# Decoder layer on one core: where three modulation segments are loaded and summed, and where the last projection group adds its partial sums

## The chip, the cores and the metric

The kernel runs on one core of one Trainium2 chip, as one launch. The time is the device time of that core in microseconds (us), the median of several runs. One further execution was recorded by the hardware profiler; the profile and the trace are of that execution.

## The reference

One layer of a decoder trunk in float32, 256 rows (tokens) of 2048 channels:

- `mod = silu(c) @ w_ada + b_ada`, cut into six segments of 2048: shift1, scale1, gate1, shift2, scale2, gate2. `w_ada` is 2048 x 12288, so one segment is 16 MB of weights for one row of result.
- `h = rms_norm(x) * (1 + scale1) + shift1`, and `proj = h @ w_in`. The columns of `proj` feed three token mixers (stick-breaking attention, dilated attention, gated linear attention, called GLA below) and three sigmoid branch gates of 2048 columns each.
- `y` = sum over the three branches of gate times (mixer output @ its branch weights); `x = x + gate1 * (y @ w_out)`.
- `h2 = rms_norm(x) * (1 + scale2) + shift2`; `x = x + gate2 * ((silu(h2 @ w_gate) * (h2 @ w_up)) @ w_ffn_out)`.

So gate1 is first needed when `y @ w_out` is there, shift2 and scale2 directly after it, gate2 at the very end.

## The kernel before

**A block.** All large products run as blocks of 512 output columns. Every float32 operand is split into a high part and a remainder, and each product is three matmuls (`mm3`, L149: high x high, high x low, low x high; their trace lines are L150, L151, L152). A block over 16 slices of 128 input channels (k) and two halves of 128 rows (t) is 96 matmuls. Its weights come in pieces of two k slices, 512 KB each (`load_weights`, L122): a DMA on SP's queue into a buffer `raw` (four of them), ScalarE (ACT) copies out the high part `whi` (L144), VectorE (DVE) subtracts for `wlo` (L145). The sums stand in the PSUM pool `acc` of four banks; a block takes two, one for each t. A second PSUM pool, `misc`, has four banks too.

**Order.** Each engine's instructions run in an order that is fixed when the kernel is built. It is set by priorities and by a modelled readiness: `prio()` (L98) moves what it holds 4000 steps ahead of its place in the program text, so weight loads, splits and evacuations of the accumulators come as soon as their buffers allow, and the blocks' matmuls fill PE's time between the matmuls of the mixers. `tc.issue_after(x)` keeps an instruction behind x on its engine. SP, ACT and DVE each work strictly through their own list; a DMA whose buffer is not free yet holds up all DMAs behind it on SP's list.

**Stages.** 36 us of start; then the first 13 blocks of `w_in` (tiles `A0` to `A12`) in four groups of k slices (`GROUPS`, L38), because the modulation (shift1, scale1) of a group of channels must be there first: in each group every block is run over that group's k alone and its sum is added to `A[b]` by DVE (`proj_block`, L386; the addition is L402). The last group has five k slices, 30 matmuls a block. Its blocks are traced in the order 0 to 4, then stick-breaking attention, then `gla()` (L532: the 16-column decay input first, in a bank of `acc`; blocks 9 to 12; the GLA chain), then blocks 5 to 8, then `dilated()` (L644). Only then comes the middle stage: two blocks for the GLA output gate, twelve gate blocks (`gate_block`, L779) and four `y_block`s (L850), then four blocks of `w_out` (the fourth with its weights kept, one t after the other, L938 to L947), then the FFN.

**The background.** The 16 MB of each later segment are streamed by a generator, `ada_segment_steps` (L307): one step issues one 512 KB load of `w_ada` into a ring buffer (`araw`), and, as many steps later as the ring has buffers, DVE multiplies that piece by silu(c) and adds it to the segment's accumulator (`ada_mac`, L242; its trace line is L247; "a mac" below). A mac is issued after the latest split that has been traced (`state["split"]`), which, as `block` traces all its splits first, is the last split of the current block. `block` calls `tick` once for every two k slices; `state["rate"]` says how many background steps a tick makes: nothing in the four groups, 0.8 in the middle stage (`RATE_MID`), 0.4 in the FFN. The background of the middle stage (L710) does gate1, then shift2, then scale2, each one whole before the next: 32 loads, then the sums over the 128 partitions on PE. For shift2 and scale2 these are 16 products with a column of ones (`column_sum`, L289, traced as L290); for gate1 (`gate_rows`, L728) the bias is added, and products with a 128 x 128 matrix of ones give every row the sum. Before the fourth `w_out` block `flush()` (L939) runs all background that is left.

Of the kernel before, what the change touches and what calls it, by code (L numbers as in the profile page):

```python
# [10 lines left out]
F32 = mybir.dt.float32  # L11
# [6 lines left out]
P = 128  # L18
T = 256
# [46 lines left out]
def trunk(ctx: ExitStack, tc: tile.TileContext, I, out):  # L66
# [38 lines left out]

    state = {"rate": 0.0}
    bg = []
    later = []

    def tick(n):  # L110
        state["due"] = state.get("due", 0.0) + n
        while state["due"] >= 1.0:
            state["due"] -= 1.0
            if bg and next(bg[0], "end") == "end":
                bg.pop()

    def flush():
        while bg:
            tick(1)


# [24 lines left out]
                parts += [(hi[:, i, :], lo[:, i, :]) for i in range(n)]  # L146
        return parts

    def mm3(ps, lh, ll, rh, rl, start, stop):  # L149
        nc.tensor.matmul(ps, lh, rh, start=start, stop=False)  # L150
        nc.tensor.matmul(ps, lh, rl, start=False, stop=False)  # L151
        state["mm"] = nc.tensor.matmul(ps, ll, rh, start=False, stop=stop)  # L152

    def block(pss, act, src, k0, k1, c0, base=0, w=None, tiles=range(NT), go_on=False, more=False):

        if w is None:
            w = load_weights(src, k0, k1, c0)
        for k in range(k0, k1):
            if (k - k0) % 2 == 0 and tiles[-1] == NT - 1:
                tick(state["rate"])  # L160
            if k - k0 == DEFER and later:
                with tc.issue_after(state["mm"].ins), prio():
                    later.pop()()
            wh, wl = w[k - k0]
            for t in tiles:
                h, l = act(base + k, t)
                mm3(pss[t], h, l, wh, wl, k == k0 and not go_on, k == k1 - 1 and not more)

    def split_from_psum(hi, lo, ps):
        nc.scalar.copy(hi, ps)  # L170
# [133 lines left out]
        ring["n"] += 1  # L304
        return S(ring["tags"][ring["n"] % len(ring["tags"])], shape, dtype)

    def ada_segment_steps(acc, seg):  # L307

        steps = [(k, j) for k in range(KC) for j in range(2)]
        lag = len(ring["tags"])  # L310
        raws = []

        def mac(i):
            k, j = steps[i]
            with tc.issue_after(state["split"].ins):
                ada_mac(acc[j], raws[i], k)

        for i, (k, j) in enumerate(steps):
            if i >= lag:
                mac(i - lag)  # L320
            raw = araw([P, 2 * NB])
            c0 = seg * D + j * 2 * NB
            with prio():
                nc.sync.dma_start(raw, w_ada[k * P : (k + 1) * P, c0 : c0 + 2 * NB])
            raws.append(raw)
            yield
        for i in range(len(steps) - lag, len(steps)):
            mac(i)
            yield


# [51 lines left out]
    orders = (up[1:] + up[:1], up, down)  # L383
    carried = []

    def proj_block(g, b, w=None, carry=False):  # L386
        k0, k1 = GROUPS[g]
        go_on = bool(carried)
        pss = carried.pop() if go_on else [acc_bank() for _ in range(NT)]
        block(pss, h_at, w_in, k0, k1, b * NB, w=w, go_on=go_on, more=carry)  # L390
        if carry:
            carried.append(pss)
            return
        with prio():
            first = A[b] is None
            if first:
                A[b] = S(f"A{b}", [P, NT, NB])
            for t in range(NT):
                if first:
                    nc.scalar.copy(A[b][:, t, :], pss[t])  # L400
                else:
                    nc.vector.tensor_add(A[b][:, t, :], A[b][:, t, :], pss[t])  # L402
# [30 lines left out]
    for g in range(len(GROUPS) - 1):  # L433
# [7 lines left out]
        for _ in nxt:  # L441
            pass
        h_group(g + 1)
    LAST = len(GROUPS) - 1


    kc = S("KC", [P, 8, P])
# [83 lines left out]

    def gla():  # L532
        aw = load_weights(w_in, 0, KC, COL_A, P)
        ps = acc_bank([P, T])
        for k in range(KC):
            hh = hT[0][k // 4][:, k % 4, :]
            hl = hT[1][k // 4][:, k % 4, :]
# [169 lines left out]
        return oT  # L707


    def background():  # L710
        state["gate1"] = yield from gate_rows(SEG_GATE1)
        state["mod2"] = []
        for seg in (SEG_SHIFT2, SEG_SCALE2):
            acc = [S(f"T{4 + j}", [P, 2 * NB]) for j in range(2)]
            yield from ada_segment_steps(acc, seg)
            v = const.tile([P, KC], F32, name=nm("mod2"))
            for i in range(0, KC, 4):
                ps = misc_bank([P, 4])
                for j in range(4):
                    q = (i + j) % 8  # L720
                    with tc.issue_after(state["mm"].ins):
                        column_sum(ps[:, j : j + 1], acc[(i + j) // 8][:, q * P : (q + 1) * P])
                    if j % 2:
                        yield
                finish_columns(ps, v[:, i : i + 4], seg, i, ROW_N2 if seg == SEG_SCALE2 else None)
            state["mod2"].append(v)

    def gate_rows(seg):  # L728
        acc = S("ada", [P, D])
        yield from ada_segment_steps([acc[:, : 2 * NB], acc[:, 2 * NB :]], seg)  # L730
        for j in range(4):
            c = slice(j * NB, (j + 1) * NB)
            br = scr([1, NB])
            nc.sync.dma_start(br, I["b_ada"][:, seg * D + c.start : seg * D + c.stop])
            nc.vector.tensor_add(acc[0:1, c], acc[0:1, c], br)
            yield
        for _ in range(4):
            yield
        for j in range(4):
            c = slice(j * NB, (j + 1) * NB)  # L740
            hl = araw([P, 2, NB], F32R)
            hi, lo = hl[:, 0, :], hl[:, 1, :]
            nc.scalar.copy(hi, acc[:, c])
            nc.vector.tensor_tensor(lo, acc[:, c], hi.bitcast(F32), op=ALU.subtract)
            yield
            ps = misc_bank([P, NB])
            with tc.issue_after(state["mm"].ins):
                nc.tensor.matmul(ps, ones_r, hi, start=True, stop=False)
                nc.tensor.matmul(ps, ones_r, lo, start=False, stop=True)
            nc.scalar.copy(acc[:, c], ps)  # L750
            yield
        return acc
# [143 lines left out]
    def residual(n, t, ps):  # L896

        xr = x2[n][:, t, :]
        tmp = scr([P, NB])
        nc.vector.tensor_mul(tmp, gate1[:, n * NB : (n + 1) * NB], ps)  # L900
# [39 lines left out]
    sh2, sc2 = state["mod2"]  # L940
# [16 lines left out]
    w_ff = I["w_ffn_in"]  # L957

    def gate2_bg():
        state["gate2"] = yield from gate_rows(SEG_GATE2)  # L960

    state["rate"] = RATE_FFN
    ring["tags"] = ("AR0", "AR1", "KC")
# [36 lines left out]
    def add_out(n, t, ps, pieces=1):  # L1000

        w = NB // pieces
        for a in range(0, NB, w):
            tmp = scr([P, w])
            c0 = n * NB + a
            nc.vector.tensor_mul(tmp, gate2[:, c0 : c0 + w], ps[:, a : a + w])
# [51 lines left out]
```

## Time and profile before

| | before |
|---|---|
| median of 3 runs | 1651.34 us (1651.2 to 1651.47) |
| profiled execution: its own time | 1653.2 us |
| profiled execution: span, first to last instruction | 1651.4 us |
| PE matmul busy | 1605.1 us, 97% of the span |
| DVE busy | 1136.2 us, 69% |
| ACT busy | 773.0 us, 47% |
| data moved | 395.91 MB, mean 240 GB/s |

A busy time is the sum of an engine's recorded instructions. PE's matmuls overlap (each is recorded as about 390 ns long, and one starts every 226 ns or so), so PE can be recorded as busy while it makes less progress than it could: the number of matmuls in a stretch is the better measure. "PEclk" is the share of full speed that PE's clock was granted. "Idle before" is the time that an engine stood still ahead of an instruction, with what ended it.

### The profile page before, as it was taken

What the parts mean: (1) busy time and instruction counts of PE and PEld (TensorE: products, weight loads), DVE (VectorE), ACT (ScalarE), POOL (GpSimd) and SP (SyncE); (2) the same over time, 40 slices, a digit from 0 to 9 for tenths busy, and PEclk for the clock granted to TensorE, in tenths of its full rate; (3) what the DMA queues carried; (4) which work ended last, traced back from release to release, by engine and by line L of the source; (5) the groups of instructions that cost most, each with busy time, mean ns of one, the idle gap of its engine ahead of it and who ended that gap; (6) DMA issues with size and microseconds to landing.
All of it is one profiled execution on the core that took longest, in us unless ns stands there. A gap on an engine that the chain in (4) does not pass through costs nothing.

```text
span 1651.4 us, 19878 instructions
## 1 busy us (share of the span) xinstructions
PE 1605.1 (97%) x7293; PEld 1324.2 (80%) x7293; DVE 1136.2 (69%) x1367; ACT 773.0 (47%) x1073; POOL 6.0 (0%) x14
## 2 busy tenths in 40 slices
PE   3999999999999999899998999999999999999998
PEld 3788888888878887688887788888888888888887
DVE  5789997787888476866987556766755555554453
ACT  5554446556755444344444644444444444433332
POOL 1000000000000000000000000000000000000000
PEclk8999999999999999999999999999999999999999
DMA  8899986445698778987997467877666566565663
GB/s 299 311 320 323 330 286 217 140 140 166 219 314 296 230 230 309 310 276 263 324 313 268 151 229 258 269 255 258 234 191 190 181 190 192 190 202 194 206 207 111
DMA packets 194561, 395.91 MB, mean 240 GB/s; under 512 B 12898, under 2 KB 27912, under 8 KB 194464
## 3 DMA queue, kind: packets, MB, share of 16 engines
q1 hardware_dynamic: 194240, 394.63, 71.9%
q8 instruction: 57, 0.93, 0.2%
q14 instruction: 40, 0.33, 0.1%
q0 software_dynamic: 224, 0.01, 0.0%
HBM read 392.50 MB, written 2.10 MB: 239 GB/s over the span
## 4 chain that ended last, share of the span: by engine, by line
PE 82%; DMA 7%; DVE 6%; issue 2%; ACT 2%; SPq 1%; DVEq 0%; ACTq 0%
PE acc L150 26%; PE acc L151 26%; PE acc L152 26%; DVE wlo L145 2%; DVE T L247 2%; DMA raw<-w_in 2%; DMA raw<-w_out 2%; ACT whi L144 1%; PE misc L592 1%; PE misc L290 1%; PE misc L846 1%; DVE ada L247 1%; DMA A<-x 1%; DMA raw<-w_br_gla 0%; DMA OS<-w_ada 0%
## 5 line engine op out<-in xcount | busy, mean ns | idle before, releaser
L145 DVE TENSOR_TENSOR wlo<-raw,whi 128x1024 fp32r<-128x1024 f32 (+1 forms) x548 | 653.3, 1197 | 422.2 <-ACT whi L144 420.1
L144 ACT CAST whi<-raw 128x1024 fp32r<-128x1024 f32 (+1 forms) x548 | 563.8, 1032 | 734.2 <-PE acc L152 555.4
L151 PE MATMUL acc<-wlo,H 128*128 128x512 f32 x1576 | 617.7, 392 | 1.7 <-DVE wlo L145 1.7
L150 PE MATMUL acc<-whi,H 128*128 128x512 f32 x1576 | 616.4, 392 | 2.5 <-ACT whi L144 2.5
L152 PE MATMUL acc<-whi,H 128*128 128x512 f32 x1576 | 616.8, 392 | 0.0
L151 PEld LDWEIGHTS acc<-wlo,H 128*128 128x128 f32 x1576 | 297.0, 189 | 64.3 <-DVE wlo L145 4.0
L150 PEld LDWEIGHTS acc<-whi,H 128*128 128x128 f32 x1576 | 296.8, 188 | 64.4 <-ACT whi L144 3.4
L152 PEld LDWEIGHTS acc<-whi,H 128*128 128x128 f32 x1576 | 296.8, 188 | 62.7 <-DVE H L372 0.9
L150 PE MATMUL acc<-whi,A 128*128 128x512 f32 x312 | 123.1, 396 | 2.7 <-ACT whi L144 2.7
L151 PE MATMUL acc<-wlo,A 128*128 128x512 f32 x312 | 123.1, 395 | 1.7 <-DVE wlo L145 1.7
L152 PE MATMUL acc<-whi,A 128*128 128x512 f32 x280 | 110.2, 394 | 0.0
L150 PEld LDWEIGHTS acc<-whi,A 128*128 128x128 f32 x312 | 59.1, 190 | 15.5 <-ACT whi L144 3.5
L151 PEld LDWEIGHTS acc<-wlo,A 128*128 128x128 f32 x312 | 59.5, 191 | 15.0 <-DVE wlo L145 2.9
L152 PEld LDWEIGHTS acc<-whi,A 128*128 128x128 f32 x280 | 53.4, 191 | 11.2
L402 DVE TENSOR_TENSOR A<-A,acc 128x512 f32<-128x512 f32 x72 | 47.9, 684 | 10.2 <-PE acc L152 10.0
L150 PE MATMUL acc<-whi,T 128*128 128x512 f32 x120 | 46.7, 389 | 0.0
L151 PE MATMUL acc<-wlo,T 128*128 128x512 f32 x120 | 46.7, 389 | 0.0
L152 PE MATMUL acc<-whi,T 128*128 128x512 f32 x120 | 46.7, 389 | 0.0
L247 DVE SCALAR_TENSOR_TENSOR ada<-AR,csil,ada 128x1024 f32<-128x1024 f32 x35 | 44.2, 1278 | 0.8 <-DMA AR<-w_ada 0.8
L152 PE MATMUL acc<-whi,OS 128*128 128x512 f32 x112 | 43.6, 389 | 0.0
L247 DVE SCALAR_TENSOR_TENSOR T<-AR,csil,T 128x1024 f32<-128x1024 f32 x30 | 38.1, 1277 | 0.0
L247 DVE SCALAR_TENSOR_TENSOR ada<-OS,csil,ada 128x1024 f32<-128x1024 f32 (+2 forms) x33 | 35.5, 1074 | 1.4 <-DMA OS<-w_ada 1.2
(323 smaller groups left out, 1198.5 us busy)
## 6 DMA issues: line engine op xcount, KB each, us to landing
raw<-w_in SPq DMA_DIRECT2D x205, 512.0 KB, 4.8
raw<-w_ffn_in SPq DMA_DIRECT2D x176, 512.0 KB, 3.7
raw<-w_ffn_out SPq DMA_DIRECT2D x88, 512.0 KB, 4.7
AR<-w_ada SPq DMA_DIRECT2D x69, 512.0 KB, 4.7
KC<-w_ada SPq DMA_DIRECT2D x35, 512.0 KB, 5.9
raw<-w_out SPq DMA_DIRECT2D x32, 512.0 KB, 7.0
KD<-w_ada SPq DMA_DIRECT2D x24, 512.0 KB, 5.6
OS<-w_ada SPq DMA_DIRECT2D x16, 512.0 KB, 6.3
```

Of the source, the lines that this page charges most:

```text
L144: nc.scalar.copy(hi[:, :n, :], raw[:, :n, :])
L145: state["split"] = nc.vector.tensor_tensor(lo[:, :n, :], raw[:, :n, :], hi[:, :n, :].bitcast(F32), op=ALU.subtract)
L150: nc.tensor.matmul(ps, lh, rh, start=start, stop=False)
L151: nc.tensor.matmul(ps, lh, rl, start=False, stop=False)
L152: state["mm"] = nc.tensor.matmul(ps, ll, rh, start=False, stop=stop)
L247: nc.vector.scalar_tensor_tensor(acc, raw, c, acc, op0=ALU.mult, op1=ALU.add)
L290: nc.tensor.matmul(ps, acc, ones[:, 0:1], start=True, stop=True)
L402: nc.vector.tensor_add(A[b][:, t, :], A[b][:, t, :], pss[t])
L592: nc.tensor.matmul(ps[:, h, :], at(lhs, h, t), at(rhs, h, t), start=True, stop=True)
L846: nc.tensor.transpose(ps[:, i, :], src[:, i * P : (i + 1) * P], ident)
```

## The change

- The background starts before the last group. Its rate is still 0 for blocks 0 to 4; from the stick-breaking attention on it is 0.8 (`RATE_IN`), which makes it run during the last group's blocks 9 to 12 and 5 to 8 with a ring of two buffers. In the middle stage, with four buffers, the rate is 0.6.
- The order is shift2, gate1, scale2, as one unbroken stream of loads: a segment's sums over partitions go into a second list, `after`, of which each tick makes a step as well, so that they run beside the next segment's loads. Column sums start four steps after the segment's last mac. gate1 and gate2 are kept as four quarters, summed in pieces of 256 columns through the tile `T6`. gate1 now stands in `T4` and `T5`, shift2 and scale2 in `ada`.
- In the last group, blocks 1 to 12 (block 0 goes on from the group before) start from their sum so far: ACT copies `A[b]` into the two PSUM banks ahead of the block ("a seed"), all matmuls accumulate onto it, and ACT copies the banks back into `A[b]`. DVE's additions of these blocks are gone.
- The decay input of `gla()` uses a bank of `misc` instead of `acc`. The first FFN block keeps its late weights in other tiles.

```diff
-RATE_MID, RATE_FFN = 0.8, 0.4
+RATE_IN, RATE_MID, RATE_FFN = 0.8, 0.6, 0.4
...
+            for work in (bg, after):
+                if work and next(work[0], "end") == "end":
+                    work.pop(0)
...
+    macs = []
+    def mac():
+        acc, j, k, raw, done = macs.pop(0)
+        with tc.issue_after(state["split"].ins):
+            ada_mac(acc[j], raw, k)
+        if done is not None:
+            after.append(done)
+    def ada_segment_steps(acc, seg, done):
+        for k in range(KC):
+            for j in range(2):
+                while len(macs) >= len(ring["tags"]):
+                    mac()
+                raw = araw([P, 2 * NB])
...
+                macs.append((acc, j, k, raw, done if (k, j) == (KC - 1, 1) else None))
+                yield
+    def last_macs():
+        while macs:
+            mac()
             yield
...
-        block(pss, h_at, w_in, k0, k1, b * NB, w=w, go_on=go_on, more=carry)
+        seeded = g == LAST and not go_on
+        if seeded:
+            with prio():
+                for t in range(NT):
+                    nc.scalar.copy(pss[t], A[b][:, t, :])
+            go_on = True
+        block(pss, h_at, w_in, k0, k1, b * NB, w=w, go_on=go_on, more=carry, seeded=seeded)
...
-                if first:
+                if first or seeded:
                     nc.scalar.copy(A[b][:, t, :], pss[t])
                 else:
                     nc.vector.tensor_add(A[b][:, t, :], A[b][:, t, :], pss[t])
...
-        ps = acc_bank([P, T])
+        ps = misc_bank([P, T])
...
+    def columns(seg, acc):
+        for _ in range(4):
+            yield
+        v = const.tile([P, KC], F32, name=nm("mod2"))
+        for i in range(0, KC, 4):
+            ps = misc_bank([P, 4])
+            for j in range(4):
+                with tc.issue_after(state["mm"].ins):
+                    column_sum(ps[:, j : j + 1], acc[:, (i + j) * P : (i + j + 1) * P])
+                if j % 2:
+                    yield
...
+    def background():
+        for seg in (SEG_SHIFT2, SEG_GATE1, SEG_SCALE2):
+            if seg == SEG_GATE1:
+                acc = [S(f"T{4 + j}", [P, 2 * NB]) for j in range(2)]
+                yield from ada_segment_steps(acc, seg, rows_of("gate1", seg, acc))
+            else:
+                acc = S("ada", [P, D])
+                yield from ada_segment_steps(halves(acc), seg, columns(seg, acc))
+        yield from last_macs()
+    bg.append(background())
     for b in range(0, 5):
         proj_block(LAST, b)
+    state["rate"] = RATE_IN
     sb_hi, sb_lo = stick_breaking()
...
-    bg.append(background())
...
-            w = load_weights(w_ff, 0, KC, 0, spare=("A12", "T4", "T5", "A9", "A10", "OD", "A1", "T1"))
+            w = load_weights(w_ff, 0, KC, 0, spare=("A12", "KD", "A9", "A10", "A0", "A1", "T1", "T2"))
```

More of the change, by code (lines that the diff above doesn't have):

```diff
@@ L113, in tick @@
             state["due"] -= 1.0
-            if bg and next(bg[0], "end") == "end":
-                bg.pop()
+            for work in (bg, after):
+                if work and next(work[0], "end") == "end":
+                    work.pop(0)
     def flush():
-        while bg:
+        while bg or after:
             tick(1)
@@ L147, in load_weights, with mm3, block @@
         return parts
[L149 to L154, printed above, removed]
+    def mm3(ps, lh, ll, rh, rl, start, stop, seeded=False):
+        nc.tensor.matmul(ps, lh, rh, start=start, stop=False, skip_group_check=seeded)
+        nc.tensor.matmul(ps, lh, rl, start=False, stop=False, skip_group_check=seeded)
+        state["mm"] = nc.tensor.matmul(ps, ll, rh, start=False, stop=stop, skip_group_check=seeded)
+    def block(pss, act, src, k0, k1, c0, base=0, w=None, tiles=range(NT), go_on=False, more=False, seeded=False):
         if w is None:
@@ L305, in araw @@
         return S(ring["tags"][ring["n"] % len(ring["tags"])], shape, dtype)
[L307 to L328, printed above, removed]
+    macs = []
[11 more added lines that the diff above has]
+                raw = araw([P, 2 * NB])
+                c0 = seg * D + j * 2 * NB
+                with prio():
+                    nc.sync.dma_start(raw, w_ada[k * P : (k + 1) * P, c0 : c0 + 2 * NB])
+                macs.append((acc, j, k, raw, done if (k, j) == (KC - 1, 1) else None))
[3 more added lines that the diff above has]
+            mac()
             yield
@@ L707, in dilated, with rows_of @@
         return oT
[L710 to L732, printed above, removed]
+    mod2 = {}
+    def columns(seg, acc):
[9 more added lines that the diff above has]
+                    yield
+            finish_columns(ps, v[:, i : i + 4], seg, i, ROW_N2 if seg == SEG_SCALE2 else None)
+        mod2[seg] = v
+    def rows_of(name, seg, acc):
+        quarters = [a[:, c : c + NB] for a in acc for c in (0, NB)]
+        for j, q in enumerate(quarters):
             br = scr([1, NB])
-            nc.sync.dma_start(br, I["b_ada"][:, seg * D + c.start : seg * D + c.stop])
-            nc.vector.tensor_add(acc[0:1, c], acc[0:1, c], br)
+            nc.sync.dma_start(br, I["b_ada"][:, seg * D + j * NB : seg * D + (j + 1) * NB])
+            nc.vector.tensor_add(q[0:1, :], q[0:1, :], br)
             yield
@@ L959, in gate2_bg @@
     def gate2_bg():
[L960 removed]
+        acc = halves(S("ada", [P, D]))
+        yield from ada_segment_steps(acc, SEG_GATE2, rows_of("gate2", SEG_GATE2, acc))
+        yield from last_macs()
     state["rate"] = RATE_FFN
```

40 lines of the change are left out of this document (22 added, 18 removed).

## The prediction

> **What bounds the kernel now.** I read the page first, then the busy time by stretches over the stages, then PE's waits.
>
> ```profile
> span 1651.4 us, 19878 instructions
> PE 1605.1 (97%) x7293; PEld 1324.2 (80%) x7293; DVE 1136.2 (69%) x1367; ACT 773.0 (47%) x1073; POOL 6.0 (0%) x14
> ```
>
> ```profile
> core 0: us, PE busy (x) PEld busy (x) DVE busy (x) ACT busy (x) POOL busy (x), PEclk, DMA share, GB/s
> 1500.00:1600.00 100.00, 100.00 (x443) 82.81 (x442) 49.94 (x45) 38.72 (x37) 0.00 (x0) 1.00 0.62 205
> 238.00:280.00 42.00, 42.00 (x196) 35.00 (x195) 35.70 (x66) 26.70 (x78) 1.75 (x1) 1.00 0.78 246
> 280.00:340.00 60.00, 60.00 (x313) 48.95 (x311) 41.18 (x75) 35.63 (x61) 0.00 (x0) 1.00 0.45 140
> 340.00:398.00 58.00, 57.88 (x321) 49.11 (x321) 54.44 (x75) 29.81 (x44) 0.00 (x0) 1.00 0.48 150
> 398.00:446.00 48.00, 47.79 (x225) 38.54 (x224) 35.54 (x93) 38.15 (x124) 0.00 (x0) 1.00 0.59 194
> 446.00:480.00 34.00, 32.41 (x156) 26.33 (x156) 29.05 (x49) 19.53 (x34) 0.00 (x0) 1.00 0.90 308
> 480.00:600.00 120.00, 120.00 (x539) 99.49 (x538) 87.97 (x92) 60.24 (x72) 0.00 (x0) 1.00 0.80 265
> 656.00:692.00 36.00, 30.50 (x123) 23.25 (x122) 30.23 (x29) 13.64 (x14) 0.00 (x0) 0.95 0.91 307
> 692.00:720.00 28.00, 27.24 (x128) 22.14 (x126) 23.54 (x24) 12.16 (x14) 0.00 (x0) 1.00 0.88 293
> 720.00:820.00 100.00, 100.00 (x462) 83.19 (x462) 72.95 (x77) 42.62 (x45) 0.00 (x0) 1.00 0.83 284
> 866.00:884.00 18.00, 14.03 (x54) 11.44 (x53) 14.20 (x12) 6.61 (x8) 0.00 (x0) 0.81 0.90 317
> ```
>
> ```profile
> PE acc L150 <- ACT whi L144: 5.1, 5, 2.4
> PE misc L290 <- DVE T L247: 4.7, 2, 4.0
> PE acc L151 <- DVE wlo L145: 3.4, 5, 1.3
> ```
>
> The kernel is bound by PE's matmul issue. In the FFN row (1500 to 1600) nothing disturbs it: 443 matmuls in 100 us, 0.226 us each, and that is the pace to compare with. Most stretches keep it. What the change can win lies only where PE loses that pace behind the start, and there are few such places. From 656 to 692 there are 123 matmuls, worth 123 x 0.226 = 27.8 us, in 36 us: **8.2 us lost**. From 692 to 720 PE is idle for 0.8 us. From 866 to 884 it is idle for 18 - 14.0 = 4.0 us, and the clock is 0.81, which is 18 x 0.19 = 3.4 us at full speed withheld; part of that falls into the idle time and into short column sums, and I count 2: **6.0 us lost**. From 446 to 480 it is idle for 1.6 us. That is 15.0 us in the three places that belong to the background (8.2 + 0.8 + 6.0), 0.9% of the span, and no change to these stages can be worth much more.
>
> **Why those three.** The ada macs of the background (L247 alone) by stretches, then SP's list:
>
> ```profile
> core 0: us, DVE busy (x), PEclk, DMA share, GB/s
> 612.00:626.00 14.00, 7.51 (x6) 1.00 0.90 306
> 626.00:636.00 10.00, 0.00 (x0) 1.00 0.87 307
> 636.00:650.00 14.00, 7.59 (x6) 1.00 0.94 326
> 650.00:660.00 10.00, 0.00 (x0) 1.00 0.79 278
> 660.00:692.00 32.00, 14.42 (x12) 0.95 0.95 322
> ```
>
> ```profile
> 669.72 0.33 SPq L324 DMA_DIRECT2D KC<-w_ada  x1
> 670.92 0.33 SPq L324 DMA_DIRECT2D KD<-w_ada  x1
> 673.25 0.33 SPq L324 DMA_DIRECT2D AR<-w_ada  x1
> 673.67 0.39 SPq L133 DMA_DIRECT2D raw<-w_br_gla  x1
> ...
> 679.54 0.94 SPq L133 DMA_DIRECT2D raw<-w_br_gla  x2
> ...
> 684.28 5.06 SPq L133 DMA_DIRECT2D raw<-w_in  x3
> ```
>
> The macs come in lumps of six, one lump per block, because each is queued behind its block's last split; each mac frees a ring buffer and a 512 KB load follows. A tick is 12 matmuls, 12 x 0.226 = 2.71 us, with one 512 KB weight piece (524,288 bytes, 193 GB/s). At 0.8 the background asks for 155 GB/s more, 348 in all; the stretches that lose pace run at 307 to 322 GB/s with the DMA engines 0.90 to 0.95 busy. Around 660 to 692 two lumps run into each other (12 macs), the weight pieces stand behind ada loads on SP's list, and PE starves. From 866 to 884 it is another thing: `flush` puts the last column sums of scale2 at a place where their macs are still running, and PE waits 4.0 us for one (the longest wait of L290 for T).
>
> **The change, part by part.** *Loads moved into the last group.* Blocks 9 to 12 and 5 to 8 have three ticks each: 24 x 0.8 = 19 of the 96 loads. They go into 280 to 398, at 140 to 150 GB/s: 19 x 0.524 MB = 10 MB over some 110 us is 90 GB/s more, 240 in all, far below the 322 seen. SP gets 19 DMAs there among the weight pieces; with two ring buffers each waits for the mac two loads back, and the weight pieces queue behind it.
>
> ```profile
> L145 DVE TENSOR_TENSOR wlo<-raw,whi 128x1024 fp32r<-128x1024 f32 (+1 forms) x548 | 653.3, 1197 | 422.2 <-ACT whi L144 420.1
> L402 DVE TENSOR_TENSOR A<-A,acc 128x512 f32<-128x512 f32 x72 | 47.9, 684 | 10.2 <-PE acc L152 10.0
> L247 DVE SCALAR_TENSOR_TENSOR ada<-AR,csil,ada 128x1024 f32<-128x1024 f32 x35 | 44.2, 1278 | 0.8 <-DMA AR<-w_ada 0.8
> L773 ACT COPY A<-acc x4: 587/589/589, 402.2 to 428.5; 128x512 f32<-128x512 f32 x4
> ACT whi L144 <- PE acc L152: 32.7, 25, 3.5
> ```
>
> *DVE in the last group* (238 to 446): 19 macs x 1.278 = +24.3 us, 24 additions x 0.684 = -16.4 us, net +8 us on 35.7 + 41.2 + 54.4 + 35.5 = 166.8 us of 208: 84% instead of 80%. The tight stretch is 340 to 398, the GLA chain, with DVE at 54.4 of 58. Macs traced there stand behind GLA in priority and can slip into 398 to 446 (35.5 of 48), and a slower chain starves nobody as long as blocks for the output gates are there to fill PE, which they are from 398 on.
>
> *Seeds.* ACT gets 24 evacuations at 0.589 (L773, the same copy from PSUM) and 24 copies of the same size into PSUM, a direction that no row shows. Bounds: at least about half of that 0.589, at most twice; I take 0.6, since size and engine are L773's. That is 24 x 1.2 = 29 us on 26.7 + 35.6 + 29.8 + 38.2 = 130.3 us, 76% of 208. On the path they cost nothing if the four copies (2.4 us) between a block's end and the start of the block after next fit into the block between, 30 x 0.226 = 6.8 us. In front of them may stand a split that waits for its buffer; the longest such wait in this stage was 3.5 us (last row above; ACT's waits, 238 to 400). 2.4 + 3.5 = 5.9 < 6.8: it fits, barely. Behind a waiting seed stand the splits and the mixers' exponentials, which PE needs. I take 0; the price without cover stands under the rivals.
>
> *Rate 0.6 in the middle stage.* Demand falls to 193 + 116 = 309 GB/s, which the old 612 to 636 stretch carried at 306 to 307 without PE losing pace; lumps shrink from 6.4 to 4.8 macs per block, and DVE from (1.197 + 0.8 x 1.278) / 2.71 = 82% to 72%. Of the 8.2 us I expect 6.2 back: lumps can still meet in the first y_block, with a quarter fewer loads in them. The 0.8 at 692 to 720 is a column sum that waits for its mac; column sums now start four steps after the last mac, 4 / 0.6 x 2.71 = 18 us: gone.
>
> *The end.* The stream is 96 loads + 4 steps for the last macs + 12 for scale2's sums = 112. Due by the end of the third `w_out` block: 19.2 + 0.6 x 144 ticks + 0.6 x 24 = 120; step 112 falls into the second. So `flush` finds nothing, no column sum waits for a mac, and `w_out` loads its weights nearly alone: the 6.0 us go. gate1's sums end near step 88, before `w_out` needs them.
>
> *The rest.* Sums in pieces of 256 columns: same columns through PE, 16 pairs instead of 8, at most 0.2 us. The decay input in `misc` holds one of the mixers' four banks while it is summed; PE has blocks to fill. The FFN's late weights get tiles that come free no later than before. All 0, within half a microsecond either way.
>
> *Sum.* -6.2 - 0.8 - 6.0 = -13.0. For new short stalls in the last group, which has more on DVE, ACT and SP than before, I add 1.5, the size of the stall at 446 to 480 (bounds 0 and 5, three such), and 0.2 for the pieces: **-11.3 us**. Span 1651.4 - 11.3 = 1640.1. The profiled execution took 1653.2, 1.8 more than its span, and the median of the runs is 1651.34, equal to the span within 0.1; so I forecast 1640.0 for the median.
>
> **The rivals.** *Order, not bandwidth (stall stays).* If 656 to 692 is lost because weight pieces stand behind ada loads on SP's list, fewer loads a tick need not help: a lump still comes before the next block's pieces. Then 8.2 stays and 0.8 + 6.0 goes, less 1.7 for new stalls: 1651.3 - 5.1 = 1646.2. For it: the pieces issued at 673.67 and 679.54 do stand behind a run of ada loads. Against it: the single lump of 612 to 626 cost nothing, nor did those of 480 to 600 (539 matmuls in 120 us); the loss comes where two meet at 322 GB/s. [...] The trace shows no more than 326 in the stretches above at 0.94 busy, so I put the limit there and the larger chance on the rate.
>
> *Slower: PE waits for seeds.* Place: the start of blocks 1 to 12. Point from which it decides: when the two evacuations and two seeds end later than 6.8 us after the block before last, for instance when two waits of 3.5 us stand in front (2.4 + 7.0 = 9.4, 2.6 us late). At 2.6 us for 12 blocks it is 31 us, at 2 us 24; less the 13.0 won: 1651.3 + 11 to 18, some 1664. For it: ACT is a strict list, 76% full, and so far DVE did these evacuations. Against it: ACT's splits run ahead of PE in the same stage, and PE was idle for 0.3 us in all from 238 to 446.
>
> *The moved loads do not run where they are traced.* With two buffers and DVE full in GLA, most of the 19 slip into the middle stage; then the stream ends 19 / 0.6 x 2.71 = 86 us later, in the third `w_out` block or at `flush`, and the 6.0 us stay lost: 1640 + 6 = 1646. Against it: each mac is tied to a split that PE needs soon.
>
> **How the numbers follow.** Likeliest case 0.57; order 0.22; moved loads slip 0.06; seeds late 0.15. What a measurement can tell from no change here is about 0.2%, 3.3 us. The likeliest case alone spans 1635 (nothing of the 15.0 left and no new stall: 1636.3, and 1.6 from 446 to 480) to 1645 (new stalls 5, 2 more left in the first y_block). The range takes in the two cases at 1646 with 3 to 4 us for their own stalls, and leaves the seeds' case out: 1634 to 1650. Faster is the first three less 0.04 that end within 0.2%: 0.81; same 0.05; slower 0.14.
>
> **What would show it.** Right: DVE's L402 rows fall from 72 to 48; macs appear from about 290 on; the middle stage runs at 300 to 310 GB/s with lumps of about five macs; no wait of L290 for L247 at the end of `w_out`; PEclk stays 1.00 behind the start; FFN blocks keep 0.226 us. Wrong: PE waiting for ACT copies of `acc<-A` from 240 to 370 (seeds); weight pieces landing late around the first y_block with PE idle (order); column sums after the third `w_out` block (slip); or a stall at GLA's end that grows with DVE's 340 to 398 share.

## The result and the profile after

The changed kernel takes 1642.15 us (median of 4 runs, 1639.62 to 1644.58), the kernel before 1651.4 us in the same comparison: ratio 0.9961, interval 0.9943 to 0.9978. It is faster by 9.25 us. The profiled execution took 1639.62 us with a span of 1637.8 us.

The changed file has other line numbers: the splits are L146 (ACT) and L147 (DVE), the three matmuls L152 to L154, DVE's addition into `A[b]` L417, the macs L249, column sums L292, the seeds L403, ACT's evacuation of the projection blocks L415. The page of the changed kernel:

```profile
span 1637.8 us, 19950 instructions
PE 1599.9 (98%) x7309; PEld 1320.3 (81%) x7309; DVE 1120.5 (68%) x1351; ACT 801.8 (49%) x1133; POOL 6.0 (0%) x14
```

Its busy time by stretches (columns as in the prediction):

```profile
280.00:340.00 60.00, 58.03 (x265) 45.04 (x265) 48.54 (x79) 43.54 (x75) 0.00 (x0) 1.00 0.75 240
480.00:600.00 120.00, 116.87 (x544) 96.68 (x543) 91.93 (x108) 53.69 (x66) 0.00 (x0) 0.99 0.85 285
656.00:692.00 36.00, 35.46 (x160) 28.98 (x159) 31.59 (x34) 16.76 (x21) 0.00 (x0) 1.00 0.89 304
692.00:720.00 28.00, 28.00 (x132) 23.15 (x131) 21.23 (x23) 14.37 (x19) 0.00 (x0) 1.00 0.81 261
866.00:884.00 18.00, 18.00 (x81) 14.92 (x80) 11.94 (x12) 9.56 (x12) 0.00 (x0) 1.00 0.71 231
```

The stall at the first y_block (160 matmuls where there were 123) and the one at the end of `w_out` (clock 1.00, nothing idle) are gone. In their place PE is idle for 2.0 us from 280 to 340 and for 3.1 us from 480 to 600, where before it never was.

**Where the time went.** Three marks can be found in both traces: the fourth group's column sums, the first y_block's turn, and norm2's first transpose. First the column sums, in the kernel before, in the changed kernel, and in a second execution of the changed kernel (the run `again` below):

```profile
241.06 1.39 PE L290 MATMUL misc<-ones,ada 128*128 128x1 f32 x12
```
```profile
236.30 1.39 PE L292 MATMUL misc<-ones,ada 128*128 128x1 f32 x12
```
```profile
238.82 1.39 PE L292 MATMUL misc<-ones,ada 128*128 128x1 f32 x12
```

Up to here PE's, DVE's and ACT's instructions are the same and in the same order in both kernels, apart from the first block's two seeds on ACT, the first of which begins at 234. The 4.8 us between the two profiled executions are therefore not the change's; two executions of one kernel differ here by 2.5 us. Next, from the column sums to the turn and from the turn to norm2, all instructions, then the third matmul of `mm3` (L152 before, L154 after) alone; before, then after:

```profile
241.06:604.40 363.34, 361.42 (x1748) 298.49 (x1747) 284.21 (x445) 210.15 (x407) 1.75 (x1) 1.00 0.67 217
604.40:908.00 303.60, 293.18 (x1312) 240.65 (x1310) 229.82 (x238) 125.32 (x141) 0.00 (x0) 0.98 0.86 292
241.06:604.40 363.34, 173.76 (x447) 1.00 0.67 217
604.40:908.00 303.60, 158.63 (x405) 0.98 0.86 292
```
```profile
236.30:607.70 371.40, 366.00 (x1770) 300.80 (x1769) 291.22 (x442) 232.86 (x450) 1.69 (x1) 1.00 0.76 245
607.70:894.10 286.40, 285.75 (x1296) 236.43 (x1294) 206.70 (x222) 130.28 (x153) 0.00 (x0) 1.00 0.80 266
236.30:607.70 371.40, 173.81 (x447) 1.00 0.76 245
607.70:894.10 286.40, 157.57 (x405) 1.00 0.80 266
```

Each stretch holds the same blocks in both kernels (447 and 405 matmuls of that line). The second is 17.2 us shorter, the first 8.1 us longer. Some small work changed sides: 32 recorded column sums of about 0.11 us went from the second stretch to the first, and gate1's sums (some 1.9 us) the other way, 1.6 us in all. So some **15.6 us were won in the middle stage and at its end, and 6.5 us lost in and behind the last group**. The rest of the kernel is equal within 0.3 us. 15.6 - 6.5 = 9.1 us agrees with the medians' 9.25. The two sizes rest on one recorded execution of each kernel; the run `again` repeats the changed kernel's stretches within 0.3 us (371.5 and 286.6), while the kernel before has no second trace.

The lines of the change itself in the trace after:

```profile
L417 DVE TENSOR_TENSOR A<-A,acc x48: 677/686/690, 105.0 to 248.2; 128x512 f32<-128x512 f32 x48
L403 ACT COPY acc<-A x24: 576/592/607, 234.1 to 335.4; 128x512 f32<-128x512 f32 x24
```

72 additions have become 48, and there are 24 seeds of 0.592 us. What PE waited for from 238 to 900 in the changed kernel (us in total, times, longest):

```profile
PE acc L153 <- DVE wlo L147: 2.6, 3, 1.0
PE misc L715 <- DVE T L711: 2.4, 1, 2.4
PE misc L940 <- DVE scr L937: 0.7, 1, 0.7
PE misc L760 <- DVE T L756: 0.5, 1, 0.5
PE misc L500 <- DVE A L493: 0.3, 1, 0.3
```

No wait for a seed is among them, and none for a column sum. The new waits are for splits that come late from DVE, and one of 2.4 us of a transpose of the dilated attention (L715) for its scaled probabilities (L711). They are not the whole 6.5 us: in the first stretch PE is idle for 5.4 us where it was idle for 1.9, and from 480 to 500 the granted clock was 0.91, worth up to 1.8 us more; the rest is in no row.

### The profile page after: what moved, and what is told of

Read it like the earlier page. It is cut to its first block, busy times and chain, and to the rows that moved or that the text cites. A ratio compares the mean times of both kernels' runs of the same rounds, so it can differ in the third digit from the quotient of the medians.

```text
span 1637.8 us, 19950 instructions
## 1 busy us (share of the span) xinstructions
PE 1599.9 (98%) x7309; PEld 1320.3 (81%) x7309; DVE 1120.5 (68%) x1351; ACT 801.8 (49%) x1133; POOL 6.0 (0%) x14
## 4 chain that ended last, share of the span: by engine, by line
PE 91%; DVE 3%; DMA 2%; ACT 2%; issue 1%; SPq 0%; DVEq 0%; ACTq 0%
PE acc L153 28%; PE acc L154 28%; PE acc L152 28%; DVE wlo L147 1%; DMA raw<-w_br_gla 1%; PE misc L606 1%; PE misc L871 1%; PE misc L292 1%; ACT whi L146 1%; DVE ada L249 1%; PE misc L366 0%; DMA A<-x 0%; PE misc L500 0%; DMA AR<-w_ada 0%; DMA raw<-w_ffn_in 0%
## 5 line engine op out<-in xcount | busy, mean ns | idle before, releaser
L147 DVE TENSOR_TENSOR wlo<-raw,whi 128x1024 fp32r<-128x1024 f32 (+1 forms) x548 | 653.4, 1198 | 435.9 <-ACT whi L146 432.6
L146 ACT CAST whi<-raw 128x1024 fp32r<-128x1024 f32 (+1 forms) x548 | 564.2, 1032 | 706.1 <-PE acc L154 556.5
L152 PE MATMUL acc<-whi,H 128*128 128x512 f32 x1576 | 615.6, 392 | 2.2 <-ACT whi L146 2.1
L154 PE MATMUL acc<-whi,H 128*128 128x512 f32 x1576 | 616.0, 391 | 0.0
L152 PEld LDWEIGHTS acc<-whi,H 128*128 128x128 f32 x1576 | 296.0, 188 | 63.4 <-ACT whi L146 3.0
L154 PEld LDWEIGHTS acc<-whi,H 128*128 128x128 f32 x1576 | 296.3, 188 | 62.2 <-DVE H L378 0.9
L152 PE MATMUL acc<-whi,A 128*128 128x512 f32 x312 | 122.3, 392 | 0.0
L154 PE MATMUL acc<-whi,A 128*128 128x512 f32 x280 | 109.1, 390 | 0.0
L249 DVE SCALAR_TENSOR_TENSOR ada<-AR,csil,ada 128x1024 f32<-128x1024 f32 x59 | 75.1, 1278 | 1.6 <-DMA AR<-w_ada 1.5
L152 PEld LDWEIGHTS acc<-whi,A 128*128 128x128 f32 x312 | 58.6, 188 | 12.0
L154 PEld LDWEIGHTS acc<-whi,A 128*128 128x128 f32 x280 | 52.5, 188 | 11.1
L152 PE MATMUL acc<-whi,T 128*128 128x512 f32 x120 | 46.8, 390 | 0.0
L154 PE MATMUL acc<-whi,T 128*128 128x512 f32 x120 | 46.7, 389 | 0.0
L154 PE MATMUL acc<-whi,OS 128*128 128x512 f32 x112 | 43.6, 389 | 0.0
L415 ACT COPY A<-acc 128x512 f32<-128x512 f32 x50 | 28.6, 586 | 21.1 <-PE acc L154 20.1
L249 DVE SCALAR_TENSOR_TENSOR ada<-OS,csil,ada 128x1024 f32<-128x1024 f32 (+2 forms) x33 | 35.5, 1075 | 0.5 <-DMA OS<-w_ada 0.2
L417 DVE TENSOR_TENSOR A<-A,acc 128x512 f32<-128x512 f32 x48 | 31.9, 684 | 5.1 <-PE acc L154 4.9
```

The lines of the kernel that those rows point to most:

```text
L146: nc.scalar.copy(hi[:, :n, :], raw[:, :n, :])
L147: state["split"] = nc.vector.tensor_tensor(lo[:, :n, :], raw[:, :n, :], hi[:, :n, :].bitcast(F32), op=ALU.subtract)
L152: nc.tensor.matmul(ps, lh, rh, start=start, stop=False, skip_group_check=seeded)
L249: nc.vector.scalar_tensor_tensor(acc, raw, c, acc, op0=ALU.mult, op1=ALU.add)
```

## The experiments

Each was timed in rounds with the kernel before, and each ratio is to the kernel before of the same rounds. My theory at the start: the rate and the stream won the middle stage and the end; the last group's loss comes from the macs that stand ahead of splits on DVE. The main rivals: ACT's 48 copies are the loss; and in the middle stage it is the order, not the rate.

**again: the changed kernel once more.**

> The changed kernel once more, nothing edited. In the profile shown, everything up to the last group (the column sums of the fourth group, 241.1 us before, 236.3 after) runs 4.8 us earlier though no engine's order of work differs up to there. Theory: that is the way this one execution's loads went, not the change; in another execution these column sums start anywhere from 236 to 241, and the ratio to the kernel before stays 0.992 to 0.998. Rival: the change itself makes the start faster; then 236 again.

1641.73 us, ratio 0.9951 (0.9939 to 0.9963). The column sums began at 238.82, so the start varies by itself, as expected. In the executions profiled it lay between 236.3 and 241.3, with the same work up to there. The kernel before alone ranged from 1644.9 to 1652.9 over many runs, so only the ratios are compared below.

**no_seed: the stream without the seeds.**

```diff
-        seeded = g == LAST and not go_on
+        seeded = False
```

> The changed kernel with the seeds taken out: blocks 1 to 12 of the last group end in VectorE's additions again (24 more rows of 0.684 us on VectorE, 48 copies less on ScalarE); the background and all else stay. Theory 1: the last group's loss (8.2 us more from 236 to the first y_block's turn than before) comes from the macs that stand ahead of splits on VectorE; then without seeds VectorE is fuller still and the time is that of the changed kernel or up to 5 us more (1642 to 1648). Rival: it comes from the 48 copies on ScalarE, ahead of which or behind which the splits stand; then the time falls by 3 to 8 us (1634 to 1639).

1647.43 us, ratio 0.9991 (0.9980 to 1.0003): 5.7 us slower than the changed kernel, which speaks against ACT's copies as the loss. What PE waited for from 280 to 400, and DVE's list at the second longest of these waits (2.1 us at 342.6; the list at the longest has the same order):

```profile
PE acc L153 <- DVE wlo L147: 5.5, 3, 2.2
```
```profile
338.96 1.29 DVE L249 SCALAR_TENSOR_TENSOR ada<-AR,csil,ada 128x1024 f32<-128x1024 f32 x1 [0.75 <-DMA AR<-w_ada]
340.16 1.28 DVE L417 TENSOR_TENSOR A<-A,acc 128x512 f32<-128x512 f32 x2
341.36 2.36 DVE L147 TENSOR_TENSOR wlo<-raw,whi 128x1024 fp32r<-128x1024 f32 x2
```

DVE stands 0.75 us for a load of `w_ada`, makes the mac, then two additions of 0.64 us each, and only then the split for which PE waits. A seed takes these additions off this list. The edit also moved GLA (its first score products began at 374, in the changed kernel at 357), so these waits need not be the whole 5.7 us.

**seed_only: the kernel before with the seeds and the other PSUM pool for the decay input.** The edit is the change's own hunks in `mm3`, `block`, `proj_block` and `gla`.

> The kernel before with the seeds alone (and the decay input's sum in the other PSUM pool, as the change has it); background, order and rates as before. Theory 1: seeds are hidden: 1651 within 2 us, and the stretch from the fourth group's column sums to the end of the dilated transposes is no longer than before (234 us). Rival: seeds cost PE at the starts of 12 blocks: 1655 to 1660. If seeds relieve VectorE where it limits the mixers, 1648 to 1650.

1652.12 us, ratio 1.0015 (1.0004 to 1.0026): about 2 us slower, at the edge of "hidden". GLA came later, though no PE wait named a seed. Since this edit has two parts, misc_only and seed_acc below separate them.

**rate08: the changed kernel at the old rate.**

```diff
-RATE_IN, RATE_MID, RATE_FFN = 0.8, 0.6, 0.4
+RATE_IN, RATE_MID, RATE_FFN = 0.8, 0.8, 0.4
```

> The changed kernel with the middle stage's rate at 0.8, as before the change; early start, one stream, order and seeds stay. If the rate is what took the stall at the first y_block away, the stall comes back somewhere in the middle stage (one or two places of 3 to 8 us, DMA at 320 GB/s and more there): 1646 to 1652. If it was the order of the segments or the unbroken stream, the time stays at 1640 to 1644 and the stream only ends some 40 us earlier.

1667.36 us, ratio 1.0103 (1.0089 to 1.0118), far worse than expected and worse than the kernel before at the same rate. Its stretches, and its longest PE wait from 238 to 900:

```profile
480.00:600.00 120.00, 111.00 (x510) 90.90 (x509) 97.56 (x120) 57.00 (x76) 0.00 (x0) 0.96 0.87 298
600.00:656.00 56.00, 51.77 (x220) 41.87 (x219) 40.01 (x40) 21.08 (x21) 0.00 (x0) 0.97 0.88 300
656.00:692.00 36.00, 34.00 (x149) 27.61 (x149) 28.16 (x25) 15.63 (x17) 0.00 (x0) 1.00 0.90 307
692.00:720.00 28.00, 23.55 (x88) 17.92 (x87) 18.23 (x17) 7.34 (x7) 0.00 (x0) 0.88 0.86 286
```
```profile
PE acc L152 <- ACT whi L146: 14.3, 4, 6.2
```

At the pace of 0.226 us the 967 matmuls of these four rows are worth 219 us; they took 240. So the stream stands or falls with the rate: one number costs 25 us. Why 0.8 costs more here than in the old order is not shown; a likely reason is that the old background issued no loads from 514 to 557 and from 729 to 759, between its segments, and here no break of the stream is longer than 19 us.

The mean bandwidth did not stop PE. These rows run at 286 to 307 GB/s with the DMA engines 0.86 to 0.90 busy, and the changed kernel's 656 to 692 ran at 304 and 0.89 and lost almost nothing. Shorter stretches carried more without loss, one in the changed kernel and one in the kernel before itself:

```profile
640.00:656.00 16.00, 16.00 (x73) 1.00 0.98 349
```
```profile
510.00:520.00 10.00, 10.00 (x45) 1.00 0.99 355
```

The 10 us from 530 to 540 of this run read 369, a row so short that its edges count, and PE lost nothing in it.

What did stop PE stands on SP's list at the longest wait (6.2 us, to 574.9). SP's list, what SP waited for from 553 to 569, and ACT's split at the end of the wait:

```profile
559.52 2.17 SPq L328 DMA_DIRECT2D AR<-w_ada  x2
...
567.30 0.33 SPq L328 DMA_DIRECT2D AR<-w_ada  x1
567.72 8.75 SPq L135 DMA_DIRECT2D raw<-w_in  x5
```
```profile
SPq L328 <- DVE T L249: 11.3, 8, 2.3
```
```profile
573.78 1.04 ACT L146 CAST whi<-raw 128x1024 fp32r<-128x1024 f32 x1 [10.37 <-DMA raw<-w_in]
```

From 556 to 567.3 SP issued seven ada loads and nothing else, and stood still for macs that had to free their buffers (11.3 us in eight waits); the weight pieces came only behind them, at 567.72, and ACT stood still for 10.4 us until the first had landed. Meanwhile (553 to 568) the DMA engines moved 298 GB/s. So at this wait it is the order of SP's list that starved PE. The place that the change was to mend shows the same in a smaller size, from 655 to 692, before and then after:

```profile
SPq L324 <- DVE T L247: 18.5, 11, 3.3
ACT whi L144 <- DMA raw<-w_br_gla: 16.4, 4, 6.8
```
```profile
SPq L328 <- DVE ada L249: 9.5, 7, 2.0
ACT whi L146 <- DMA raw<-w_br_gla: 7.5, 4, 4.0
```

A lower rate helps, as I read these lines, because fewer ada loads, with fewer waits for macs, stand ahead of the pieces.

**in0: no background in the last group.**

```diff
-RATE_IN, RATE_MID, RATE_FFN = 0.8, 0.6, 0.4
+RATE_IN, RATE_MID, RATE_FFN = 0.0, 0.7, 0.4
```

> The changed kernel with no background in the last group (rate 0 there) and 0.7 in the middle stage, so that the stream still ends before the fourth w_out block (0.7 x 168 ticks = 117.6 of 112 steps). Theory: the last group's loss is the macs' together with the seeds', and the middle stage's stalls follow the rate. Then the stretch from the fourth group's column sums to the first y_block's turn falls from 371 us to about 368, what the seeds alone measured, and the middle stage (203.5 us from the first to the fourth turn at 0.6) loses 3 to 8 us at 0.7, between 0.6 (no stall over 1.1 us) and 0.8 (about 20 us): 1643 to 1649. Rival, the order and not the rate: middle stage as at 0.6, total 1637 to 1640.

1644.48 us, ratio 0.9979 (0.9969 to 0.9990). The total lies where the theory put it, the reason does not. The stretch from the column sums to the first turn took 372 us, not 368, and the stretch behind it 288.6 us where the changed kernel took 286.4: the middle stage lost some 2 us at 0.7, not 3 to 8. Its longest waits from 238 to 900:

```profile
PE misc L715 <- DVE T L711: 2.6, 1, 2.6
PE acc L153 <- DVE wlo L147: 2.1, 4, 0.8
```

The wait of the dilated transposes is as long with no mac in the last group as with 19. My theory of the last group's loss fell here: without any mac in that group the stretch is no shorter.

**misc_only: the kernel before with the decay input in the other pool.**

```diff
-        ps = acc_bank([P, T])
+        ps = misc_bank([P, T])
```

> The kernel before with the decay input of GLA summed in the other PSUM pool and nothing else. With the seeds alone GLA's first score products began at 358 us, before at 344, and the last group lost 4.6 us. If the pool is the reason, GLA begins at 355 or later here too, and the time is 1651 to 1655, that of the seeds alone (1.0015 of before). If the copies on ScalarE are, GLA begins at 344 to 348 and the time is that of before within 1 us.

1651.75 us, ratio 1.0025 (1.0015 to 1.0034): this one line costs 4 us by the medians. When the decay input was copied out (the copy `aT`), and GLA's first scored level, in the kernel before and in this one:

```profile
L540 ACT COPY scr<-acc x1: 356/356/356, 329.6 to 329.6; 16x256 f32<-16x256 f32 x1
L592 PE MATMUL misc<-T x112: 271/275/348, 349.3 to 391.6; 128*128 128x128 f32 x112
```
```profile
L540 ACT COPY scr<-misc x1: 359/359/359, 340.3 to 340.3; 16x256 f32<-16x256 f32 x1
L592 PE MATMUL misc<-T x112: 270/275/348, 357.3 to 394.1; 128*128 128x128 f32 x112
```

Before, the 48 products of the decay input ran from 282 to 291, between the first heads of the stick-breaking attention; in the other pool they ran from 334 to 340, behind its last head, and in every other kernel with this line later still, from 338 to 358 on. GLA and the dilated attention begin some 8 and 14 us later, and PE waits where they then meet other work (1.8 us for L697's probabilities, 1.3 us at the turn of GLA's output). I had expected GLA at 355 or later by its first score products; they began at 350. The trace does not show where the 4 us lie: against the one trace of the kernel before, the first stretch is 2.5 us longer (365.7), but the second 2.9 us shorter (300.7). Beside the stream it is clearer (the last table of this section).

**before085: the old background a little faster, so that nothing is left for the flush.**

```diff
-RATE_MID, RATE_FFN = 0.8, 0.4
+RATE_MID, RATE_FFN = 0.85, 0.4
```

> The kernel before with its rate in the middle stage at 0.85 in place of 0.8: 0.85 x 168 ticks = 142.8, so that all 140 background steps are made before the flush ahead of the fourth w_out block. Tests the end by itself. Theory: the wait of the last column sums at the flush (4.0 us and the half clock behind it, 6.0 us in all) goes, and the middle stage has as much or more stall than before: from the fourth turn to the first norm2 transposes 84 to 87 us in place of 91.3, total 1646 to 1652. Rival: what ends there is the loads and not the place of the sums; then that stretch stays at 90 or more.

1652.95 us, ratio 1.0035 (1.0023 to 1.0048). The wait of the last column sums fell from 4.0 to 0.5 us, but from the fourth turn to norm2 it still took 90.4 us, because loads now starved PE there:

```profile
820.00:866.00 46.00, 42.58 (x188) 34.33 (x187) 35.95 (x38) 16.14 (x19) 0.00 (x0) 0.96 0.87 301
```

So the end of the wait for the sums won nothing at this rate. It fits that the changed kernel wins its end because the stream is over before `w_out` needs its weights; but the edit also raised the rate, and no run moves the sums alone.

**in04: half the background in the last group.**

```diff
-RATE_IN, RATE_MID, RATE_FFN = 0.8, 0.6, 0.4
+RATE_IN, RATE_MID, RATE_FFN = 0.4, 0.65, 0.4
```

> The changed kernel with half the background in the last group (rate 0.4) and 0.65 in the middle stage (9.6 + 0.65 x 168 = 118.8 of 112 steps). A split between the two stages. If both losses are proportional to their rates, the last group gains 1 to 2 us and the middle stage loses 1 to 3: 1640 to 1645. If the middle stage has a threshold above 0.65, only the gain stays: 1638 to 1641, better than the changed kernel.

1637.74 us, ratio 0.9944 (0.9932 to 0.9956), with no PE wait over 0.9 us from 238 to 900. Its median lies below both ends, 0 (in0) and 0.8, which speaks against losses proportional to the rates. Against in0 the intervals are apart; against `again` they overlap.

**acc_after: the changed kernel with the decay input back in the accumulators' pool.**

```diff
-        ps = misc_bank([P, T])
+        ps = acc_bank([P, NB])
...
+            if k == 0:
+                nc.tensor.matmul(ps, aw[k][0], hT[0][0][:, 0:2, :].rearrange("p a t -> p (a t)"), start=True, ...)
...
```

That the first product covers the whole bank was my precaution for the seeds that follow in this pool. No run has a half-wide sum in `acc` beside seeds, so it is not shown that it is needed; nor is it shown that such a need was why the change moved the sum.

> The changed kernel with the decay input of GLA summed in the accumulators' pool again, as before the change (its first product is taken over 512 columns, 0.1 us more, so that a seed may follow in that bank); seeds, rates and stream stay. In the changed kernel this sum runs from 339 us on, before from 282 on, and GLA and the dilated tail come some 13 and 20 us later. Theory: the pool makes the sum wait for the stick-breaking attention's banks, that is worth 2.5 to 4 us as in the run with the pool alone (1.0025 of before): the sum runs near 285, GLA starts at 343 to 350, total 1637 to 1640 against 1642 for the changed kernel (ratio 0.992 to 0.9935). Rival: the last group's loss is the macs' place alone; then GLA starts earlier and the ratio stays at 0.995 to 0.996.

1637.82 us, ratio 0.9939 (0.9927 to 0.9951). The sum ran from 278 to 286 again, and the time is where expected (the ratio is just above the 0.992 to 0.9935 that was named). GLA, however, still began at 358 and not at 343 to 350: what keeps GLA late here is not the pool alone.

**acc_in04: both repairs.**

> Both cheap repairs: the decay input in the accumulators' pool and the rates 0.4 in the last group, 0.65 in the middle stage, everything else as changed. If the two are independent, the ratio is that of the rates (0.9944) less 0.0015 to 0.0025: 0.992 to 0.993, and no stall over 1 us is left between 240 and 890 us. If they cure the same stall (the dilated products that wait for VectorE near 485), 0.994 to 0.995.

1638.34 us, ratio 0.9939 (0.9927 to 0.9951). The two do not add up, and the hope that no stall over 1 us is left between 240 and 890 failed at two waits; the ratio lies nearer to the case that both cure the same stall:

```profile
PE misc L765 <- DVE T L761: 1.3, 1, 1.3
PE misc L720 <- DVE T L716: 1.1, 1, 1.1
```

GLA began at 346 here, where only the rates differ from acc_after, so its lateness there came with the rate of 0.8. The three runs in04, acc_after and acc_in04 beat the kernel before; their medians also lie below the changed kernel's two ratios, 0.9951 and 0.9961, but the intervals overlap, and among the three nothing can be told apart.

**acc_no_seed: the early stream alone.**

> The early stream alone: the changed kernel without seeds (VectorE adds again) and with the decay input in the accumulators' pool, as before. Without seeds but in the other pool it was 0.9991 of before. Theory: the pool is worth as much here, 0.995 to 0.9965, so that the seeds, for which the pool was changed, pay only for their own move. Rival: with the macs beside it VectorE is the limit in the last group and only the seeds relieve it; then 0.998 to 1.000 here too.

1642.3 us, ratio 0.9965 (0.9952 to 0.9978): the upper end of the theory's range. **seed_acc: the seeds alone**, the kernel before with the seeds and with the decay input's sum as in acc_after:

> The kernel before with the seeds alone and the decay input left in the accumulators' pool (first product over 512 columns). Closes the table of pool, seeds and stream. The pool alone measured 1.0025 of before, pool and seeds 1.0015. Theory: without the stream VectorE is not the limit, so seeds alone gain next to nothing: 0.998 to 1.000 of before. If the seeds are a gain of their own, as large as beside the stream (0.9939 against 0.9965): 0.9965 to 0.998. If they cost what the pair's 1.0015 suggested: above 1.000.

1650.28 us, ratio 1.0009 (0.9998 to 1.0021), nearest to the third case, with 1 inside the interval: neither a gain nor a cost is shown. That closes the table (ratio to the kernel before):

| | old background | early stream, 0.8 and 0.6 |
|---|---|---|
| no seeds, pool `acc` | 1 | 0.9965 |
| no seeds, pool `misc` | 1.0025 | 0.9991 |
| seeds, pool `acc` | 1.0009 | 0.9939 |
| seeds, pool `misc` | 1.0015 | 0.9951 and 0.9961 (the change) |

The stream wins some 0.35% without seeds and 0.5 to 0.7% with them. The seeds win nothing that can be measured by themselves, and 0.26 to 0.4% beside the stream; the likely reason is that only then is DVE's list full enough for two additions to hold up a split, as at the waits of no_seed. The other pool costs some 0.25% without seeds, with either background; with seeds (0.06 to 0.2%) the intervals overlap.

The two stretches between the marks, each from one profiled execution (rate08 is left out: its first turn comes only at 732.6, so that its stretches hold other blocks):

| us | column sums to first turn | turn to norm2 |
|---|---|---|
| kernel before | 363.3 | 303.6 |
| misc_only | 365.7 | 300.7 |
| seed_only | 367.7 | 297.5 |
| seed_acc | 364.3 | 302.6 |
| before085 | 363.0 | 305.8 |
| the change, and again | 371.4, 371.5 | 286.4, 286.6 |
| no_seed (pool `misc`) | 374.2 | 286.8 |
| acc_no_seed | 370.9 | 286.0 |
| acc_after | 367.4 | 286.0 |
| in04 (pool `misc`) | 366.1 | 286.5 |
| acc_in04 | 365.8 | 288.1 |

With the stream at 0.8 and 0.6 the second stretch is the same within 0.8 us, and the first says what the pool costs: 3.3 us without seeds, 4.0 with them. At the rate of 0.4 it is 0.3 us: pool and rate seem to cure the same loss, so neither has a price of its own.

## Why the prediction was right

*Forecast 1640.0, range 1634 to 1650, faster: measured 1642.15.* The direction and the places were those of the likeliest case. That the total came within 2.2 us is partly luck: 2.6 us more were won in the middle stage and at the end than forecast, 5.0 more were lost in the last group.

*Middle stage and end, -13.0 forecast: some -15.6 measured.* The 8.2 us at the first y_block came back almost whole (35.46 of 36 us busy), not 6.2 of it. `flush` had nothing left, and no column sum waited, as worked out from the steps. That the end comes from the stream being over, more than from the place of the sums, I had named but given no weight; before085 speaks for it. What failed here is my reason for the first place: a limit near 326 GB/s. The kernel before itself ran at 355 from 510 to 520 and lost nothing.

*New stalls in the last group, +1.5 forecast (0 to 5): some +6.5 measured.* This step failed, beyond its bound. Inside it, the decay input in `misc`, which I had put at 0, was a wrong entry: in the other pool the changed kernel's first stretch is 4.0 us shorter (acc_after). I counted the bank that the sum holds, not that it would run some 50 us later and push GLA and the dilated attention back. The remaining 2.5 us are not settled. PE's recorded waits are for splits behind macs and for the dilated products near 485, but in0, without macs in the group, has the dilated wait too (2.6 us). DVE's 84% on average said nothing about what stands ahead of what.

*Seeds, 0 forecast: 0 on PE's path.* Each took 0.592 us against the 0.6 assumed, and the five waits above show none for them. DVE's 16.4 us of additions I had counted as relief off the path; beside the stream they are worth 0.26 to 0.4%.

*Of the rivals.* Seeds late: not seen. Moved loads slip: they ran where traced; 16 macs lie between 290 and 398. Order, not bandwidth: the stall did go, so as a forecast this rival lost, but its cause was the right one: in rate08 PE starved at 298 GB/s behind seven ada loads on SP's list. It failed in saying that fewer loads a tick need not help. What decides between a harmless lump and a stall was not settled; no run changed the order of loads at an unchanged rate.

*The span.* The profiled execution's span gained 13.6 us, 4.8 of them ahead of the change. By that span alone the forecast of 1640.1 would look too timid, for a wrong reason.

## What to carry to other kernels

At 0.8 the unbroken stream took 1.0103 of the time of the kernel before, whose background ran at the same 0.8 with pauses; at 0.6 it took 0.9951 and 0.9961. So set a background's rate anew when its pauses go. In the changed kernel the last mac of the stream comes before 800 us and PE did not stand still from 866 to 884; in the kernel before, macs were still running there and PE stood still for 4.0 of these 18 us. So try to have a stream end before the next stage loads its weights. An edit that looks like housekeeping, here the pool of one small sum, can move that sum by 50 us; look in the trace at what then comes later and what it meets there. The seeds won nothing that can be measured alone and 0.26 to 0.4% beside the stream, so try relief for an engine beside the load that fills its list too, not only alone.

## What the runs showed of the hardware

The first 240 us took 236.3 to 241.3 us in different executions of the same PE and DVE instructions. Most of that arises before 94 us, with the DMA engines 0.89 to 0.92 busy: by then 282 matmuls had been recorded in the kernel before and 297 in the changed kernel; from 94 on PE hardly stood still (141.8 to 142.0 of 142 us busy). Single spans of this kernel cannot be compared below 5 us.

The mean GB/s did not tell whether PE starved: 349 over 16 us went without loss (the changed kernel, 640 to 656), while a wait of 6.2 us came with 298 over 15 us (rate08, 553 to 568).

In the changed kernel ACT's copy of 128 x 512 from SBUF into PSUM took 0.592 us (median of the 24 at L403), from PSUM into SBUF 0.589 us (of the 50 at L415). The two differ in source and in destination, and no run changes one alone.
